# A hybrid decoder layer on one core: operand preparation moved between pairs, and a norm factor computed on GpSimd

## The chip, the cores and the metric

The kernel runs on one core of one Trainium2 chip. The metric is the device time of one execution in microseconds, and the time of a kernel is the median of several runs. A profiled execution is taken beside the timed runs; its trace gives the start and the duration of each instruction on each engine: PE (TensorE matmuls), PEld (TensorE weight loads), DVE (VectorE), ACT (ScalarE), POOL (GpSimd) and SP (SyncE, which only issues transfers here).

## The reference, cut to what matters

One layer over 1024 tokens of width 1024, all in float32. Three root-mean-square norms stand inside it and one behind it; between the first projection and `w_out` lie a pooling mixer and a gated recurrence, which the change doesn't touch:

```
def rms_norm(x, g):
    xf = x.astype(jnp.float32)
    y = xf * lax.rsqrt(jnp.mean(xf * xf, axis=-1, keepdims=True) + RMS_EPS)
    return (y * g.astype(jnp.float32)).astype(x.dtype)

z = rms_norm(h, norm_mix_g[l]);  proj = z @ w_in[l]
...
h = h + jnp.concatenate([y_pool, y_lru], axis=-1) @ w_out[l]
z = rms_norm(h, norm_mlp_g[l])
h = h + jnp.square(jax.nn.relu(z @ w_up[l])) @ w_down[l]
z = rms_norm(h, norm_ple_g[l])
gate = jax.nn.sigmoid(z @ w_ple_gate[l] + b_ple_gate[l])
h = h + gate * (p[l] @ w_ple_proj[l])
return rms_norm(h, norm_final_g)
```

## The kernel before, in words

Activations lie transposed: 128 features on the partitions, 1024 tokens along a row, in eight row blocks `H[0]` to `H[7]`. Each float32 product is made of three matmuls: every operand is split into a high part and a low part (`split`, L189 on ACT for the high part, L190 on DVE for the low part), and high by high, high by low and low by high are accumulated (`mm`, matmuls at L447).

**The up projection** uses a fast matrix multiplication with seven products (named P1 to P7) per pair of output blocks, `m` = 0 to 15 being the pairs. From pair 4 on, two of the seven products are themselves replaced by a second level of the same scheme, over two neighbouring pairs: `up_double(m, k)`, whose small products are issued by `sub_product` (L1020), with names `ps_z_u`, `ps_v_u` and `ps_x_u`. The second level needs sums and differences of quarters of its second operand. They depend on the tokens only, so each is made once: `double_operand(k, n)` builds number `n` for product `k`, with three additions of 128x512 on DVE (L983, L986, inside `total`) and a split. For `k` = "P2" number 2 goes on from the result of number 1, number 4 from that of number 2, and number 3 stands alone; their tiles are `y_wide` (number 4) and `x` (the others). The table `MADE` (L1099) says in which pair each number is made:

```
MADE = {"P4": {1: (3,), 2: (1, 2), 3: (4,)}, "P2": {3: (3, 1), 4: (2, 4)}}
```

`double_operands(m)` is called once in each pair and reads it. The weights of a pair are split one after another ahead of their products: tiles `wu_P` (first level) and `wu_d` and `wu_l` (second level). `wu_sums_raw` holds sums of weights.

**The gate stage** behind the down projection (products `ps_P_d`) works on the first 512 tokens, then on the second 512. Product `o` of the gate is 24 matmuls (`ple_gate`, tile `ps_e`), its projection 6 (`ple_proj`, tile `ps_j`, or a second half of `ps_e`). `ple_out` multiplies the gate product by the norm's factor `R` (tile `rstd`, L1455), applies a sigmoid on ACT (L1456), multiplies by the projection (L1459), and adds to `H[o]` (L1460).

**The norms** (class `Norm`): `add` squares a block on ACT (L491) and adds it up on DVE (L492). `gather` transposes the sums on DVE (L506), reduces them (L507) and splits the result into a high and a low part (L508, L509, tile `sums`). `sums` adds them over the partitions with one small matmul (L519). `rstd` makes the factor from it: a copy and an addition on DVE (L528, L529), a square root on ACT (L533), a reciprocal on DVE (L534) and a transposition that spreads the factor over the tile `rstd` (L535). The norm of the gate has two halves: `first_sums` for the first 512 tokens (matmul result `n_ps`), and the call at L1661 for the second (`n2b_ps`), issued in the round of the gate's product 3. `finish` does the last norm of the first 512 tokens.

**The last norm of the second 512 tokens** is computed by blocks of 128 tokens. There the factor is made by GpSimd's power: `inverse` raises a 128x1 tile to -0.5 (L1590).

The order of the work on each engine is set when the kernel is built: a scheduler lists the instructions by priority, and each engine then runs its own list strictly in that order, waiting on semaphores. `tc.issue_after(ins)` keeps the scheduler from placing an instruction before another one; `pin` and `keep_in_program_order` keep written order.

Of the kernel before, what the change touches and what calls it, by code (L numbers as in the profile page):

```python
# [8 lines left out]
F32 = mybir.dt.float32  # L9
# [3 lines left out]
ALU = mybir.AluOpType  # L13

P = 128
# [49 lines left out]
def block_kernel(  # L65
# [17 lines left out]
    nc = tc.nc  # L83
    pool = ctx.enter_context(tc.tile_pool(name="pool", bufs=1))
# [4 lines left out]
    def fixed(name, dt):  # L89
        return pool.tile([P, S], dt, name=name)  # L90
# [23 lines left out]
    R = fixed("rstd", F32)  # L114
# [17 lines left out]
    spread = edge.tile([P, 72], F32, name="edge")  # L132
# [29 lines left out]
    def turns(z):  # L162
        return z.rearrange("p (a j) -> p j a", a=2)
# [11 lines left out]
    def col(name, i):  # L175
        c = COLS[name] + i
        return vecs[:, c : c + 1]
# [255 lines left out]
    def weights():  # L433
        ask()
        return asked.pop(0)

    def mm(parts, whi, wlo, zhi, zlo, first, last, only=None, more=False, held=False):
        outs = [
            (slice(hs.start + n, hs.start + min(n + HALF, w)), ps[:, n : min(n + HALF, w)])
            for hs, ps in parts  # L440
            for w in (hs.stop - hs.start,)
            for n in range(0, w, HALF)
            if only is None or hs.start + n == only.start
        ]
        for w, z in ((whi, zhi), (whi, zlo), (wlo, zhi)):
            for hs, ps in outs:
                ins = nc.tensor.matmul(  # L447
                    ps, w, turns(z[:, hs]),
                    start=first and z is zhi and w is whi,
                    stop=last and w is wlo,  # L450
                    skip_group_check=more,
                )
                if held:
                    tc.keep_in_program_order(ins)
                    held = False
# [17 lines left out]
    same = pool.tile([P, P], F32R, name="same")  # L473
    eps = pool.tile([P, 1], F32, name="eps")
    nc.scalar.activation(eps, one[:, :1], AF.Copy, scale=EPS)

    class Norm:

# [41 lines left out]
            in_order.clear()  # L520
            return [(hs, o)]

        def rstd(self, out, parts, square=False):


            for hs, o in parts:
                few = self.few(hs)
                nc.vector.tensor_copy(few, o[:, :16])  # L528
                nc.vector.tensor_tensor(few, few, o[:, 16:], ALU.add)  # L529
                if square:  # L530
                    nc.vector.tensor_scalar(few, few, 1.0 / D, EPS, ALU.mult, ALU.add)
                else:
                    nc.scalar.activation(few, few, AF.Sqrt, bias=eps, scale=1.0 / D)  # L533
                nc.vector.reciprocal(few, few)  # L534
                nc.vector.transpose(out[:, hs], few.unsqueeze(2).broadcast_to([P, 16, 32]))  # L535

    def tables():
# [45 lines left out]
    norm = Norm("n0", T[0], T[1:3])  # L583
# [6 lines left out]
    for k in range(NT):  # L590
# [41 lines left out]
        if k < 2:  # L632

            zhi, zlo = A[k]
            for hs in HALVES:
# [4 lines left out]
                for n, o in kinds:  # L640
                    w, z = ((whi, zhi), (whi, zlo), (wlo, zhi))[n]
                    at, ps = next(x for x in places[o] if x[0].start <= hs.start < x[0].stop)
                    ps = ps[:, hs.start - at.start :][:, :HALF]
# [159 lines left out]
    ps = project(3)  # L803
# [4 lines left out]
    ps = project(4)  # L808
# [3 lines left out]
    ps = project(5)  # L812
# [15 lines left out]
    norm = Norm("n1", T[4], T[5:])  # L828
# [10 lines left out]
    for o in range(NT):  # L839
# [15 lines left out]
        ps = out_ps[o]  # L855
# [240 lines left out]
        finish_up(m, cc)  # L1096
        leave_up()

    MADE = {"P4": {1: (3,), 2: (1, 2), 3: (4,)}, "P2": {3: (3, 1), 4: (2, 4)}}  # L1099

    def double_operands(m):

        for k, ns in MADE.items():
            for n in ns.get(m, ()):
# [272 lines left out]
    Z, ple, late, quad = [], [], [], []  # L1377
# [26 lines left out]
    norm2 = Norm("n2", T[0], T[1:2])  # L1404
# [2 lines left out]
    open_proj()  # L1407

    def first_sums(norm=norm2):
        norm.rstd(R, norm.sums(FIRST, pinned=True))  # L1410

    norm2 = Norm("n2b", T[0], T[1:3])


    fin = Norm("n3", T[0], T[1:3])
    rfin = T[5]
    gate_p, held = {}, []
    ms = spread[:, 40 : 40 + 4 * NTOK]
    early_mean, means, inverses = ([ms[:, 4 * x + i : 4 * x + i + 1] for i in range(NTOK)] for x in range(3))
    power = pool.tile([P, 1], F32, name="power")  # L1420
    tc.keep_in_program_order(nc.vector.memset(power, -0.5))

    def ple_psum(g, hs, o, apart):
        turn.append(o)
# [45 lines left out]
    def finish(os):  # L1470

        if 0 in os:
            fin.rstd(rfin, fin.sums(FIRST, fin.tmp[0][:, FIRST]))
        for o in os:
            hv = H[o][:, FIRST]
            nc.vector.scalar_tensor_tensor(hv, hv, col("g_fin", o), rfin[:, FIRST], ALU.mult, ALU.mult)
            if o % 4 == 3:
                store(slice(o - 3, o + 1))

    row = t_all[:, 1:3].rearrange("p a s -> p (a s)")  # L1480
    g_row, b_row, square = row[:, :S], row[:, S : S + NQUAD], row[:, S + NQUAD :]
# [147 lines left out]
    for g, hs in enumerate(GROUPS):  # L1629
        if g == 1:  # L1630
            leave("ple")
            late[:] = space("late", 8, F32)
        for n, o in enumerate(ORDER[g]):
            pg, pj = ple_psum(g, hs, o, False)
            if g == 0 and n < 2:
                ple_gate(g, hs, o, pg, n == 1)
                held.append((o, pg, pj))
                if n == 0:
                    first_sums()
                    continue  # L1640
                for o, pg, pj in held:
                    ple_proj(hs, o, pj)
                for o, pg, pj in held:
                    ple_out(hs, o, pg, pj)
            else:
                ple_proj(hs, o, pj)
                ple_gate(g, hs, o, pg)
            if g == 0 and 1 <= n < 5:
                raw = wp.tile([P, S], F32, tag="raw", name=f"wg0_{n + 3}_raw")
                nc.sync.dma_start(raw, w_gate[n + 3])  # L1650
                x = slice((n - 1) * P, n * P)
                split(raw.rearrange("p (k x) -> p k x", k=NT), *(w[:, :, x] for w in quad))
            if g > 0 or n > 1:
                ple_out(hs, o, pg, pj, g == 0)
            if g == 0 and n > 0:
                for o in range(NT) if n == 1 else ():
                    norm2.add(H[o], SECOND)
                if n == 2:
                    norm2.gather(SECOND, T[2][:, SECOND])
                if n == 3:  # L1660
                    norm2.rstd(R, norm2.sums(SECOND))  # L1661
                for o in LATER[n - 1]:
                    ple_in_normed(o, SECOND)
            if g == 1:
                for j in range(2):
                    turn_block(o, j)
                if n < 2:
                    for x in range(4, NT):
                        turn_block(x, n)
                    turn_out(1, n)  # L1670
                    for i in range(2):
                        turn_in(1, 2 * n + i)
                if n == 3:
                    for j in range(2):
                        turn_out(0, j, (nc.sync, nc.scalar)[j])
                    for i in range(NTOK):
                        turn_in(0, i)
                finish(DONE[n])
                if n == 1:
                    nc.sync.dma_start(row[:, : S + NQUAD], rows.broadcast_to([P, S + NQUAD]))  # L1680
# [127 lines left out]
```

## Time and profile before

| | us |
|---|---|
| median of 3 runs (lowest, highest) | 913.8 (913.64, 914.05) |
| profiled execution | 914.14 |
| its span in the trace | 912.4 |
| PE busy | 903.5 (99%) |
| DVE busy | 742.0 (81%) |
| ACT busy | 517.3 (57%) |
| POOL busy | 51.8 (6%) |

The span is the time from the first to the last instruction of the trace; the profiled execution is 1.74 us longer than its span. A row of the timeline gives start, duration, engine, line, operation, output<-input, the shape, a count where neighbouring instructions are merged, and in brackets the idle time of the engine ahead of the instruction with what ended it. Instructions of one engine overlap a little: a duration includes the run-out of the pipeline, so the pace of an engine is read from the starts. Starts show 0.60 us per 128x512 addition on DVE where the row says 0.68 or 0.69.

### The profile page before, as it was taken

What the parts mean: (1) busy time and instruction counts of PE and PEld (TensorE: products, weight loads), DVE (VectorE), ACT (ScalarE), POOL (GpSimd) and SP (SyncE); (2) the same over time, 40 slices, a digit from 0 to 9 for tenths busy, and PEclk for the clock granted to TensorE, in tenths of its full rate; (3) what the DMA queues carried; (4) which work ended last, traced back from release to release, by engine and by line L of the source; (5) the groups of instructions that cost most, each with busy time, mean ns of one, the idle gap of its engine ahead of it and who ended that gap; (6) DMA issues with size and microseconds to landing.
All of it is one profiled execution on the core that took longest, in us unless ns stands there. A gap on an engine that the chain in (4) does not pass through costs nothing.

```text
span 912.4 us, 11874 instructions
## 1 busy us (share of the span) xinstructions
PE 903.5 (99%) x4419; PEld 792.5 (87%) x4419; DVE 742.0 (81%) x1015; ACT 517.3 (57%) x688; POOL 51.8 (6%) x76
## 2 busy tenths in 40 slices
PE   9999999999999999999999999999999999999996
PEld 7888888888888899999998888888888888888886
DVE  7999974668977987887887978699787679899876
ACT  6569892447565666766767554463443436475323
POOL 4300001000000000000000000000001001100001
PEclk9999999999999999999999999999999999999999
DMA  7311145435477488687684988456635355332353
GB/s 274 103 47 34 59 153 148 151 92 173 117 217 225 125 246 203 194 242 198 190 243 170 352 322 285 146 193 207 199 111 145 116 173 117 57 115 70 99 170 136
DMA packets 60330, 150.90 MB, mean 165 GB/s; under 512 B 5360, under 2 KB 10352, under 8 KB 60272
## 3 DMA queue, kind: packets, MB, share of 16 engines
q1 hardware_dynamic: 54288, 136.77, 45.6%
q0 software_dynamic: 4752, 12.59, 8.3%
q10 hardware_dynamic: 1232, 0.79, 0.4%
q8 instruction: 35, 0.57, 0.2%
q14 instruction: 23, 0.19, 0.1%
HBM read 110.27 MB, written 39.85 MB: 165 GB/s over the span
## 4 chain that ended last, share of the span: by engine, by line
PE 92%; DVE 4%; issue 2%; DMA 1%; ACT 0%; POOLq 0%; POOL 0%; ACTq 0%; DVEq 0%
PE ps_P_d L447 31%; PE ps_i L447 9%; PE ps_o L447 9%; PE ps_d_u L447 8%; PE ps_b_u L447 8%; PE ps_a_u L447 5%; PE ps_e L447 5%; PE ps_z_u L1020 3%; PE ps_l L447 3%; PE ps_P_u L447 3%; PE ps_e L1541 2%; PE ps_v_u L1020 2%; PE ps_l L644 1%; PE ps_x_u L1020 1%; PE ps_g L713 1%
## 5 line engine op out<-in xcount | busy, mean ns | idle before, releaser
L447 PE MATMUL ps_P_d<-a,wd_P_hi 128*128 128x512 f32 x880 | 261.7, 379 | 0.0
L447 PEld LDWEIGHTS ps_P_d<-a,wd_P_hi 128*128 128x128 f32 x880 | 166.3, 189 | 23.6
L447 PE MATMUL ps_P_d<-a,wd_P_lo 128*128 128x512 f32 x440 | 166.8, 379 | 0.0
L447 PEld LDWEIGHTS ps_P_d<-a,wd_P_lo 128*128 128x128 f32 x440 | 83.2, 189 | 11.8
L447 PE MATMUL ps_b_u<-a,wu_P 128*128 128x512 f32 x360 | 82.6, 379 | 0.0
L222 DVE TENSOR_TENSOR t_h<-t_h 128x512 f32<-128x512 f32 (+2 forms) x104 | 72.6, 708 | 11.6 <-ACT t_h L925 10.4
L190 DVE TENSOR_TENSOR wu_P<-t_h,wu_P 128x512 fp32r<-128x512 f32 x84 | 57.4, 686 | 27.8 <-ACT wu_P L189 27.6
L447 PEld LDWEIGHTS ps_b_u<-a,wu_P 128*128 128x128 f32 x360 | 66.4, 189 | 8.4
L190 DVE TENSOR_TENSOR a<-wd,a 128x1024 fp32r<-128x1024 f32 x56 | 67.3, 1220 | 2.6 <-ACT a L189 2.3
L447 PE MATMUL ps_i<-a,wi_hi 128*128 128x512 f32 x256 | 66.1, 381 | 0.0
L189 ACT ACTIVATE wu_P<-t_h 128x512 fp32r<-128x512 f32 x84 | 52.2, 624 | 22.3 <-DVE t_h L222 11.9
L189 ACT ACTIVATE a<-wd 128x1024 fp32r<-128x1024 f32 x56 | 58.6, 1052 | 10.0 <-PE ps_P_d L447 6.5
L899 DVE TENSOR_TENSOR t_h<-t_h,ps_P_d 128x512 f32<-128x512 f32 (+1 forms) x48 | 37.1, 773 | 30.5 <-PE ps_P_d L447 30.5
L447 PE MATMUL ps_a_u<-y_wide,wu_P 128*128 128x512 f32 x240 | 55.1, 379 | 0.0
L447 PEld LDWEIGHTS ps_i<-a,wi_hi 128*128 128x128 f32 x256 | 48.1, 189 | 8.0 <-PE ps_g L713 0.3
L189 ACT ACTIVATE wd_P_hi<-wd 128x1024 fp32r<-128x1024 f32 x24 | 25.3, 1055 | 50.2 <-PE ps_P_d L447 47.7
L447 PEld LDWEIGHTS ps_a_u<-y_wide,wu_P 128*128 128x128 f32 x240 | 45.3, 189 | 6.4
L447 PE MATMUL ps_d_u<-a,wu_P 128*128 128x512 f32 x180 | 41.6, 380 | 0.1
L447 PE MATMUL ps_d_u<-y,wu_P 128*128 128x512 f32 x180 | 41.3, 379 | 0.0
L447 PE MATMUL ps_i<-a,wi_lo 128*128 128x512 f32 x128 | 38.1, 379 | 0.0
L190 DVE TENSOR_TENSOR wd_P_lo<-wd,wd_P_hi 128x1024 fp32r<-128x1024 f32 x24 | 29.3, 1221 | 10.1 <-ACT wd_P_hi L189 10.1
L447 PEld LDWEIGHTS ps_d_u<-a,wu_P 128*128 128x128 f32 x180 | 33.1, 189 | 4.7 <-DVE wu_P L190 0.5
(307 smaller groups left out, 1749.8 us busy)
## 6 DMA issues: line engine op xcount, KB each, us to landing
wd<-act SPq DMA_DIRECT2D x56, 512.0 KB, 5.5
act<-t_h SPq DMA_DIRECT2D x48, 512.0 KB, 4.9
t_h<-in_w_up SPq DMA_DIRECT2D x30, 512.0 KB, 5.0
wd<-in_w_down SPq DMA_DIRECT2D x16, 512.0 KB, 5.8
t_h<-in_w_up POOLq DMA_DIRECT2D x15, 512.0 KB, 7.8
t_h<-in_xT SPq DMA_DIRECT2D x14, 512.0 KB, 4.6
wg_raw<-in_w_gate SPq DMA_DIRECT2D x10, 512.0 KB, 3.3
wi_raw<-in_w_in SPq DMA_DIRECT2D x9, 512.0 KB, 3.3
```

Source lines behind the costliest of these rows:

```text
L189: first = pin(nc.scalar.activation(hi, src, AF.Copy))
L190: lowest[:] = [pin((eng or nc.vector).tensor_tensor(lo, src, f32(hi), ALU.subtract)).ins]
L222: return nc.vector.tensor_tensor(to, x, y, op).ins
L447: ins = nc.tensor.matmul(ps, w, turns(z[:, hs]), start=first and z is zhi and w is whi, stop=last and w is wlo, skip_group_check=more,)
L644: nc.tensor.matmul(ps, kblk(w, o), turns(z[:, hs]), start=k == n == 0, stop=False)
L713: nc.tensor.matmul(x, w[r, o * P : (o + 1) * P], turns(z[r, at : at + HALF]), start=n == 0, stop=n == 2)
L899: (eng or nc.vector).tensor_tensor(to, to if y is None else y, x, ALU.add)
L1020: nc.tensor.matmul(ps, kblk(w, t), turns(z[:, t]), start=t == x == 0 and not more, stop=t == 1 and x == 2, skip_group_check=more,)
L1541: nc.tensor.matmul(pg, z, turns(quad[x == 1][:, k]), start=n == 0, stop=n == 3 * NT - 1, skip_group_check=True)
```

## The change

Three edits.

1. In `MADE`, the operands for "P2" are made in pairs 2, 3 and 4 (number 3; then 1 and 2; then 4), where they were made in pairs 3 and 4 (3 and 1; then 2 and 4). P4's are unchanged.
2. `rstd` gets a switch `late`, used for both halves of the gate's norm and for the last norm's first half. With it the factor is not made by ACT's square root and DVE's reciprocal but by one DVE instruction (multiply and add, 128x16) and GpSimd's power with exponent -0.5 (128x16). The exponents stand in sixteen columns that GpSimd fills at the start; the single column that DVE filled at L1421 is gone.
3. The matmul of the second half's sums is held behind the last matmul that had been written so far, the last one of the gate's product 3 (the fourth gate product).

```diff
+    latest = []
@@ mm
                     skip_group_check=more,
                 )
+                latest[:] = [ins.ins]
                 if held:
@@ setup
+    powers = spread[:, 53:69]
+    nc.gpsimd.memset(powers, -0.5)
@@ Norm
-        def rstd(self, out, parts, square=False):
+        def rstd(self, out, parts, square=False, late=False):
             for hs, o in parts:
                 few = self.few(hs)
                 nc.vector.tensor_copy(few, o[:, :16])
                 nc.vector.tensor_tensor(few, few, o[:, 16:], ALU.add)
-                if square:
+                if square or late:
                     nc.vector.tensor_scalar(few, few, 1.0 / D, EPS, ALU.mult, ALU.add)
                 else:
                     nc.scalar.activation(few, few, AF.Sqrt, bias=eps, scale=1.0 / D)
-                nc.vector.reciprocal(few, few)
+                if late:
+                    nc.gpsimd.tensor_tensor(few, few, powers, ALU.pow)
+                else:
+                    nc.vector.reciprocal(few, few)
                 nc.vector.transpose(out[:, hs], few.unsqueeze(2).broadcast_to([P, 16, 32]))
@@
-    MADE = {"P4": {1: (3,), 2: (1, 2), 3: (4,)}, "P2": {3: (3, 1), 4: (2, 4)}}
+    MADE = {"P4": {1: (3,), 2: (1, 2), 3: (4,)}, "P2": {2: (3,), 3: (1, 2), 4: (4,)}}
@@ gate stage
-        norm.rstd(R, norm.sums(FIRST, pinned=True))
+        norm.rstd(R, norm.sums(FIRST, pinned=True), late=True)
-    power = pool.tile([P, 1], F32, name="power")
-    tc.keep_in_program_order(nc.vector.memset(power, -0.5))
+    power = powers[:, :1]
@@ finish
-            fin.rstd(rfin, fin.sums(FIRST, fin.tmp[0][:, FIRST]))
+            fin.rstd(rfin, fin.sums(FIRST, fin.tmp[0][:, FIRST]), late=True)
@@ round of product 3
-                    norm2.rstd(R, norm2.sums(SECOND))
+                    with tc.issue_after(latest[0]):
+                        ps = norm2.sums(SECOND)
+                    norm2.rstd(R, ps, late=True)
```

The edits move instructions in three places. In the changed kernel the lines up to L434 keep their numbers and the later ones are a few higher (L986 is L994, L492 is L497, L509 is L514, L535 is L543).

**Place 1: DVE in pair 4**, from the low part of P5's weight (`wu_P_2373`, in the changed kernel `wu_P_2378`) to the sums of weights. L986 and L994 are operand additions, L222 additions on weights, `x` the low part of an operand, `wu_d` the low part of a second-level weight. Before:

```order
L190 TENSOR_TENSOR wu_P_2373<-t_h,wu_P_2373 128x512
L986 TENSOR_TENSOR t_h<-t_h,y_wide 128x512
L222 TENSOR_TENSOR t_h<-t_h 128x512
L986 TENSOR_TENSOR t_h<-t_h,y_wide 128x512
L222 TENSOR_TENSOR t_h<-t_h 128x256
L190 TENSOR_TENSOR wu_P_2409<-t_h,wu_P_2409 128x512
L190 TENSOR_TENSOR x_1776<-t_h,x_1776 128x512
L190 TENSOR_TENSOR wu_d_2392<-t_h,wu_d_2392 128x512
```

With the change:

```order
L190 TENSOR_TENSOR wu_P_2378<-t_h,wu_P_2378 128x512
L994 TENSOR_TENSOR t_h<-t_h,y_wide 128x512
L222 TENSOR_TENSOR t_h<-t_h 128x512
L222 TENSOR_TENSOR t_h<-t_h 128x256
L190 TENSOR_TENSOR x_1778<-t_h,x_1778 128x512
L222 TENSOR_TENSOR t_h<-t_h 128x256
L190 TENSOR_TENSOR wu_P_2414<-t_h,wu_P_2414 128x512
L190 TENSOR_TENSOR wu_d_2397<-t_h,wu_d_2397 128x512
```

One operand addition is gone from between the two weights, and an addition of 128x256 that stood behind `wu_d` has come ahead of it.

**Place 2: DVE at the first half's factor.** `edge` holds the 16 sums, `wg_2_lo` and `a` are low parts of gate weights. Before:

```order
L528 COPY edge<-n_ps_6529 128x16
L190 TENSOR_TENSOR wg_2_lo<-wg_2_raw,wg_2_hi 128x1024
L529 TENSOR_TENSOR edge<-edge,n_ps_6529 128x16
L190 TENSOR_TENSOR a<-wg_4_raw,a 128x8x128
L492 TENSOR_TENSOR t_h<-t_h 128x512
L534 RECIPROCAL edge<-edge 128x16
L492 TENSOR_TENSOR t_h<-t_h 128x512
L535 STREAM_TRANSPOSE rstd<-edge 128x512
L492 TENSOR_TENSOR t_h<-t_h 128x512
L1455 TENSOR_TENSOR t_h<-ps_e_0_6497,rstd 128x512
```

With the change:

```order
L533 COPY edge<-n_ps_6528 128x16
L190 TENSOR_TENSOR wg_2_lo<-wg_2_raw,wg_2_hi 128x1024
L534 TENSOR_TENSOR edge<-edge,n_ps_6528 128x16
L190 TENSOR_TENSOR a<-wg_4_raw,a 128x8x128
L536 TENSOR_SCALAR edge<-edge 128x16
L497 TENSOR_TENSOR t_h<-t_h 128x512
L543 STREAM_TRANSPOSE rstd<-edge 128x512
L497 TENSOR_TENSOR t_h<-t_h 128x512
L1462 TENSOR_TENSOR t_h<-ps_e_0_6496,rstd 128x512
```

One addition of squares stands between the new instruction and the transposition, which waits for GpSimd's power; the addition that stood in the old gap comes later.

**Place 3: DVE and PE at the second half's sums.** On DVE, before:

```order
L1455 TENSOR_TENSOR t_h<-ps_e_2_6609,rstd 128x512
L506 STREAM_TRANSPOSE t_h<-t_h 128x512
L507 TENSOR_REDUCE edge<-t_h 128x16
L1459 TENSOR_TENSOR t_h<-t_h,ps_j_2_6610 128x512
L508 CAST sums_6229<-edge 128x16
L1460 TENSOR_TENSOR t_h<-t_h 128x512
L509 TENSOR_TENSOR sums_6229<-edge,sums_6229 128x16
L190 TENSOR_TENSOR a<-wg_6_raw,a 128x8x128
L492 TENSOR_TENSOR t_h<-t_h 128x512
```

With the change:

```order
L1462 TENSOR_TENSOR t_h<-ps_e_2_6608,rstd 128x512
L497 TENSOR_TENSOR t_h<-t_h 128x512
L511 STREAM_TRANSPOSE t_h<-t_h 128x512
L1466 TENSOR_TENSOR t_h<-t_h,ps_j_2_6609 128x512
L512 TENSOR_REDUCE edge<-t_h 128x16
L1467 TENSOR_TENSOR t_h<-t_h 128x512
L513 CAST sums_6230<-edge 128x16
L190 TENSOR_TENSOR a<-wg_6_raw,a 128x8x128
L497 TENSOR_TENSOR t_h<-t_h 128x512
L514 TENSOR_TENSOR sums_6230<-edge,sums_6230 128x16
```

The low part of the sums, which the small matmul reads, now stands behind a split of a gate weight and one more addition of squares. On PE, before (the last matmul of gate product 3, the small matmul, the first of projection 4):

```order
L447 MATMUL ps_e0_3_6661<-ple6_6239,wg0_3_lo_6619 128x512
L447 MATMUL ps_e0_3_6661<-ple6_6239,wg0_3_hi_6618 128x512
L447 MATMUL ps_e0_3_6661<-ple7_6240,wg0_3_hi_6618 128x512
L447 MATMUL ps_e0_3_6661<-ple6_6239,wg0_3_lo_6619 128x512
L519 MATMUL n2b_ps512_6708<-sums1_6229,same_162 128x32
L447 MATMUL ps_j0_4_6722<-proj0_6475,proj4_6479 128x512
```

With the change:

```order
L449 MATMUL ps_e0_3_6660<-ple6_6240,wg0_3_lo_6618 128x512
L449 MATMUL ps_e0_5_6768<-proj0_6476,proj4_6480 128x512
L449 MATMUL ps_e0_5_6768<-proj1_6477,proj4_6480 128x512
L449 MATMUL ps_e0_5_6768<-proj0_6476,proj5_6481 128x512
L449 MATMUL ps_e0_5_6768<-proj2_6478,proj6_6482 128x512
L449 MATMUL ps_e0_5_6768<-proj3_6479,proj6_6482 128x512
L524 MATMUL n2b_ps512_6707<-sums1_6230,same_162 128x32
L449 MATMUL ps_j0_4_6721<-proj0_6476,proj4_6480 128x512
```

Five of the six matmuls of projection 5 now stand between the last matmul of gate product 3 and the small matmul.

## The prediction

> **What bounds the kernel now.** I read the head of the page, then the waits of TensorE, then the timeline around each wait, then the chain of waits.
>
> ```profile
> span 912.4 us, 11874 instructions
> PE 903.5 (99%) x4419; PEld 792.5 (87%) x4419; DVE 742.0 (81%) x1015; ACT 517.3 (57%) x688; POOL 51.8 (6%) x76
> ...
> PE ps_l L589 <- PEq L1794: 0.8, 1, 0.8
> PE n2b_ps L519 <- DVE sums L509: 0.6, 1, 0.6
> PE ps_z_u L1020 <- DVE wu_d L190: 0.2, 1, 0.2
> ```
>
> TensorE sets the end. Its whole waiting is three waits: the start, which the change leaves alone, and one at each place that the change touches. The matmul count stays, so only these two waits and the hidden losses beside them can move the time. Pair 4 loses more than its row of 0.2 says:
>
> ```profile
> 294.34 2.75 PE L447 MATMUL ps_a_u<-y_wide,wu_P 128*128 128x512 f32 x12
> ...
> 297.60 3.13 PE L447 MATMUL ps_d_u<-a,wu_P 128*128 128x512 f32 x12
> ...
> 301.29 0.49 PE L1020 MATMUL ps_z_u<-x,wu_d 128*128 128x256 f32 x2
> ...
> 302.25 0.71 PE L1020 MATMUL ps_z_u<-x,wu_d 128*128 128x256 f32 x4 [0.25 <-DVE wu_d L190]
> ...
> 305.17 0.83 PE L1020 MATMUL ps_x_u<-a,wu_d 128*128 128x256 f32 x6
> ...
> 313.03 2.75 PE L447 MATMUL ps_a_u<-y_wide,wu_P 128*128 128x512 f32 x12
> ```
>
> and in the chain of waits the same product of the next two pairs (start, length):
>
> ```profile
> 313.19 2.59 PE ps_a_u L447 x12
> ...
> 330.83 2.59 PE ps_a_u L447 x12
> ```
>
> From one `ps_a_u` to the next, pair 4 takes 313.03 - 294.34 = 18.69 us, the next pair 330.83 - 313.19 = 17.64 us. So pair 4 loses 1.05: 0.38 in `ps_d_u` (3.13 against 2.75), 0.62 from 301.29 to 305.17 (3.88 us for six small matmuls at 0.112 and twelve at 0.216, 3.26), the rest beside them.
>
> The gate stage, around the second half's sums:
>
> ```profile
> 821.06 0.59 PE L447 MATMUL ps_e<-ple,wg_hi 128*128 128x512 f32 x2
> ...
> 826.99 0.28 PE L519 MATMUL n2b_ps<-sums,same 128*128 128x32 f32 x1 [0.58 <-DVE sums L509]
> 827.12 1.54 PE L447 MATMUL ps_j<-proj,proj 128*128 128x512 f32 x6
> 828.50 0.81 PE L447 MATMUL ps_e<-ple,a 128*128 128x512 f32 x3
> ```
>
> Gate product 3 is 24 matmuls at 0.216, so it is through at 821.06 + 5.18 = 826.24. The small matmul starts at 826.99: TensorE loses 0.75 there, and with the small matmul itself 0.97 (828.50 - 826.24, less 1.29 for projection 4). What it waits for is VectorE, which works through its list here without a gap:
>
> ```profile
> 805.08 4.63 DVE L190 TENSOR_TENSOR proj<-t_h,proj 128x1024 fp32r<-128x1024 f32 x4 [1.12 <-ACT proj L189]
> ...
> 809.66 0.06 DVE L1421 MEMSET power<- 128x1 f32 x1
> ...
> 810.86 0.17 DVE L529 TENSOR_TENSOR edge<-edge,n_ps 128x16 f32<-128x16 f32 x1
> 810.94 1.22 DVE L190 TENSOR_TENSOR a<-wg_raw,a 128x1024 fp32r<-128x1024 f32 x1
> 812.07 0.68 DVE L492 TENSOR_TENSOR t_h<-t_h 128x512 f32<-128x512 f32 x1
> 812.67 0.25 DVE L534 RECIPROCAL edge<-edge 128x16 f32<-128x16 f32 x1
> 812.84 0.65 DVE L492 TENSOR_TENSOR t_h<-t_h 128x512 f32<-128x512 f32 x1
> ...
> 826.77 0.17 DVE L509 TENSOR_TENSOR sums<-edge,sums 128x16 fp32r<-128x16 f32 x1
> 826.85 1.23 DVE L190 TENSOR_TENSOR a<-wg_raw,a 128x1024 fp32r<-128x1024 f32 x1
> 827.99 0.68 DVE L492 TENSOR_TENSOR t_h<-t_h 128x512 f32<-128x512 f32 x1
> ```
>
> The reader is to see that no row after 805.08 carries an idle time: from there to the sums at 826.94 VectorE is the chain, and anything put ahead of the sums makes TensorE's wait longer by its whole length.
>
> **Edit 1, the operands: -0.14.** Place 1 in the order shows what counts. The loss in `ps_d_u` hangs on P5's weight:
>
> ```profile
> 288.74 1.42 DVE L222 TENSOR_TENSOR t_h<-t_h 128x512 f32<-128x512 f32 x2 [1.39 <-ACT t_h L925]
> ...
> 297.56 0.69 DVE L190 TENSOR_TENSOR wu_P<-t_h,wu_P 128x512 fp32r<-128x512 f32 x1
> ...
> 301.51 0.68 DVE L190 TENSOR_TENSOR wu_d<-t_h,wu_d 128x512 fp32r<-128x512 f32 x1
> ```
>
> VectorE last stands idle ahead of 288.74 (for ScalarE's squares, which the edit doesn't touch). From there to P5's weight its list has the same fourteen instructions before and with the change, another operand's addition taking the place of the one moved forward. The weight comes at 297.56 again, and the 0.38 stays. Between it and `wu_d` an operand addition (0.60) leaves and a 128x256 addition (0.34) enters: `wu_d` comes 0.26 sooner. The matmuls that wait for it start at 301.99; four small ones (0.45) and now twelve of `ps_b_u` (2.59; one of them used to fill the gap) end at 305.03, against 305.17: 0.14 gained. The work moved forward, three additions and a split, lands in pair 2's end and pair 3's start, where VectorE is busy 13.07 of 18.10 us:
>
> ```profile
> 276.20:294.30 18.10, 18.10 (x85) 15.86 (x84) 13.07 (x21) 10.56 (x17) 0.88 (x1) 1.00 0.71 204
> ```
>
> The third busy number is VectorE's: 5 us are free, so the move costs nothing there. Bounds: 0, and the whole loss of 1.05.
>
> **Edits 2 and 3, the second sums: +0.51 and a wait for the power.** Place 3: five matmuls of projection 5 stand ahead of the small matmul, so TensorE reaches it at 826.24 + 1.08 = 827.32. On VectorE the split of a gate weight (826.85 to 827.99, 1.14) and one more addition of squares (0.60) now stand ahead of the sums; the reciprocal (0.17) and the memset (0.06) are gone, the multiply-and-add (0.08, as L529's start to the next) is new. Net 1.59, so the sums end at 826.94 + 1.59 = 828.53, and TensorE, 0.05 later (826.94 to 826.99 now), has waited 1.26 instead of 0.75: +0.51. That is without any wait in place 2.
>
> In place 2 VectorE has only one addition (0.60) to do between the multiply-and-add and the transposition that needs the power. The multiply-and-add starts at 812.05 (812.07 less the memset's 0.02), ends at 812.22 like other 128x16 instructions, and VectorE is free for the transposition at 812.05 + 0.08 + 0.60 = 812.73. No row shows a power of 16 columns. Those of one column are:
>
> ```profile
> 892.38 0.69 DVE L1527 TENSOR_TENSOR late<-late,t_h 128x512 f32<-128x512 f32 x1
> ...
> 892.54 0.95 POOL L1590 TENSOR_TENSOR edge<-edge,power 128x1 f32<-128x1 f32 x1 [99.84 <-DVE edge L1517]
> ...
> 901.94 0.55 POOL L1590 TENSOR_TENSOR edge<-edge,power 128x1 f32<-128x1 f32 x1 [4.45 <-DVE edge L1517]
> ```
>
> and a plain two-input instruction of four columns:
>
> ```profile
> 14.40 0.20 POOL L564 TENSOR_TENSOR sp<-sp 128x4 f32<-128x4 f32 x1
> ```
>
> A power takes 0.55, and 0.95 with a VectorE addition beside it, as there will be here. With 0.08 to reach POOL and 0.04 back, 812.22 + 0.08 + 0.95 + 0.04 = 813.29: VectorE stands for 0.56 even if fifteen more columns are free. At the other end every column costs what one costs beyond a plain instruction, 0.55 - 0.20 = 0.35, and the wait is 0.56 + 15 x 0.35 = 5.8. Part of the 0.35 is surely paid once per instruction; I take a sixth of it, 0.06 per column, nearer to the low end because four plain columns together take 0.20: a wait of 0.56 + 0.90 = 1.46. All of it delays the sums.
>
> [...]
>
> **What costs nothing, and its cover.** ScalarE loses three square roots and five of six table loads:
>
> ```profile
> 810.33 1.28 ACT L533 ACT_TABLE_LOAD   x1
> 811.63 0.31 ACT L533 ACTIVATE edge<-edge,eps 128x16 f32<-128x16 f32 x1
> ```
>
> But the root was ready at 811.94 and the reciprocal came at 812.67: VectorE's list was the limit, and nothing is gained. The second half's power leaves VectorE standing some 2 us. What hides it is the distance to the second half's operands: the last split of them, and the first product that reads them, and further down the user of two late loads:
>
> ```profile
> 850.78 0.69 DVE L190 TENSOR_TENSOR a<-t_h,a 128x512 fp32r<-128x512 f32 x1
> ```
> ```profile
> 854.56 11.65 PE ps_e L447 x54
> ```
> ```profile
> 900.31 0.69 DVE L1587 TENSOR_TENSOR late<-late,t_h 128x512 f32<-128x512 f32 x1
> ```
>
> That is 3.8 us, and more for the last of the operands, which the product reads last. Without that cover it would cost the 2 us. At the last norm a weight split and a product (1.8 us) stand between the multiply-and-add and the transposition, and TensorE doesn't wait for it. There the output's first store gets ahead of two loads on SP's queue, which then wait for four scalings; their user is the row at 900.31, so some 20 us remain. The memset on POOL at the start is 0.1 to 0.2 us on an engine that then waits for others.
>
> **The sum**: -0.14 + 0.51 + 1.46 = +1.83. The profiled execution would be 914.14 + 1.83 = 916.0; the median shown is 0.34 below the profiled execution, so I state the median: 913.8 + 1.8 = **915.6**.
>
> **The rivals.**
>
> *The power is light*: fifteen columns cost nearly nothing. For it: four columns of a product take 0.20. Against it: a single column of power takes 0.35 more than that. Time: +0.51 + 0.56 - 0.14 = +0.9, 914.7; decided by a power of 128x16 under 1.25 us.
>
> *The power is heavy*, slower: GpSimd works column by column at more than 0.10. For it, the 0.35 of one column. Place: the transposition in place 2 and through it the small matmul. From 0.10 on the wait is over 2.06 and the time over 913.8 + 2.4 = 916.2; at 0.25 it is 918.5.
>
> *The sums are in time*: VectorE reaches them before TensorE reaches 827.32, because ScalarE, free of table loads, lets VectorE run faster, and pair 4's loss vanishes whole. Time: -1.05 - 0.75 = -1.8, 912.0; with only the second part 913.0. Against it: VectorE's rows have no gap that ScalarE could close, and its list is longer by 1.59.
>
> **Chances.** Forecast (0.02 to 0.10 per column, +1.2 to +2.4) 0.45; light 0.22; heavy 0.22; in time 0.11. A measurement of this kernel can tell about 0.2%, 1.83 us, from no change, and the forecast sits on that line: half of it counts as slower. Slower 0.22 + 0.22 = 0.44; within 0.22 + 0.22 + 0.06 = 0.50; faster 0.06, half of the last rival. The range: 914.0 below (the light power with part of pair 4's loss regained), 918.5 above (0.25 per column).
>
> **What would show it.** Right: the wait of `n2b_ps` for VectorE grows from 0.6 to about 2.7; an idle time of VectorE of about 1.5 ahead of the first `rstd` transposition, released by POOL; a power of 128x16 of 1.5 to 2 us; `ps_d_u` of pair 4 still at 3.1. Wrong: no wait at `n2b_ps`, or a pair 4 of 17.64.

## The result and the profile after

The change made the kernel slower, by far more than predicted.

| | before | changed |
|---|---|---|
| median of the runs (lowest to highest, number) | 913.72 us (913.57 to 914.05, 4) | 920.63 us (919.76 to 921.10, 4) |
| ratio, 95% interval | | 1.0074 (1.0057 to 1.0092) |
| profiled execution, its span | 914.14, 912.4 | 920.78, 918.8 |

Predicted were 915.6 and a range of 914.0 to 918.5; 44% stood on slower by over 0.2%.

The waits of TensorE in the changed kernel (total, how often, the longest):

```profile
PE n2b_ps L524 <- DVE sums L514: 4.3, 1, 4.3
...
PE ps_z_u L1028 <- DVE wu_d L190: 0.4, 1, 0.4
```

The wait at the second half's sums went from 0.6 to 4.3. The timeline of TensorE shows it, and a second loss behind it:

```profile
826.21 1.24 PE L449 MATMUL ps_e<-proj,proj 128*128 128x512 f32 x5
831.71 0.39 PE L524 MATMUL n2b_ps<-sums,same 128*128 128x32 f32 x1 [4.26 <-DVE sums L514]
831.94 2.91 PE L449 MATMUL ps_j<-proj,proj 128*128 128x512 f32 x6
834.64 6.94 PE L449 MATMUL ps_e<-ple,a 128*128 128x512 f32 x24
841.42 0.38 PE L449 MATMUL ps_e<-proj,proj 128*128 128x512 f32 x1
841.63 5.34 PE L449 MATMUL ps_e<-ple,a 128*128 128x512 f32 x24
```

Six matmuls of a projection take 2.70 (834.64 - 831.94) where they took 1.38 before, and the next gate product 6.78 (841.42 - 834.64) where the one after it takes 5.18. The windows of the same trace say why; the last but two number of a row is TensorE's granted clock, the share of its full clock that it was given:

```profile
830.00:831.00 1.00, 0.00 (x0) 0.00 (x0) 1.00 (x2) 0.41 (x1) 0.00 (x0) 1.00 0.00 0
831.00:832.00 1.00, 0.29 (x2) 0.29 (x2) 1.00 (x3) 0.00 (x0) 0.00 (x0) 0.52 0.18 20
832.00:833.00 1.00, 1.00 (x4) 0.82 (x4) 0.68 (x4) 0.71 (x1) 0.17 (x1) 0.50 0.84 229
...
837.00:838.00 1.00, 1.00 (x4) 0.80 (x4) 1.00 (x3) 0.25 (x1) 0.00 (x0) 0.57 0.00 0
838.00:839.00 1.00, 1.00 (x6) 0.89 (x5) 1.00 (x3) 0.97 (x2) 0.00 (x0) 1.00 0.00 0
```

The clock fell to one half shortly after 831.0, while TensorE stood still, and came back before 838.0. In windows of 0.1 us the mean is 0.68 from 831.00 to 831.10 and 0.69 from 837.80 to 837.90, so the edges lie at 831.04 and 837.86: 6.83 us, and TensorE worked in 6.15 of them (from 831.71) at half speed.

The sum of the loss: the small matmul starts 831.71 - 826.99 = 4.72 later, of which five projection matmuls (1.08) are work done early: 3.64. From 831.71 to the 24 matmuls at 841.63 lie the small matmul (0.13 at full clock, as from 826.99 to 827.12 before) and 31 others (6.70), which would have ended at 838.54: 3.09 lost to the clock, and half of the 6.15 is 3.08. Pair 4 gives 0.03 back. Together 6.70, against 920.78 - 914.14 = 6.64.

What made the sums late is in VectorE's timeline:

```profile
812.03 0.17 DVE L536 TENSOR_SCALAR edge<-edge 128x16 f32<-128x16 f32 x1
812.11 0.69 DVE L497 TENSOR_TENSOR t_h<-t_h 128x512 f32<-128x512 f32 x1
815.63 0.71 DVE L543 STREAM_TRANSPOSE rstd<-edge 128x512 f32<-128x512 f32 x1 [2.84 <-POOL edge L540]
...
819.77 0.69 DVE L497 TENSOR_TENSOR t_h<-t_h 128x512 f32<-128x512 f32 x1
820.60 0.69 DVE L1466 TENSOR_TENSOR t_h<-t_h,ps_j 128x512 f32<-128x512 f32 x1
...
831.48 0.17 DVE L514 TENSOR_TENSOR sums<-edge,sums 128x16 fp32r<-128x16 f32 x1
```

and GpSimd's:

```profile
812.28 3.31 POOL L540 TENSOR_TENSOR edge<-edge 128x16 f32<-128x16 f32 x1 [19.62 <-DVE edge L536]
832.83 2.91 POOL L540 TENSOR_TENSOR edge<-edge 128x16 f32<-128x16 f32 x1 [17.23 <-DVE edge L536]
873.62 2.89 POOL L540 TENSOR_TENSOR edge<-edge 128x16 f32<-128x16 f32 x1 [37.88 <-DVE edge L536]
```

The power of 16 columns takes 2.9 to 3.3 us, and VectorE stands 2.84 ahead of the transposition. The sums start 831.48 - 826.77 = 4.71 later: 1.59 from the longer list, as predicted; 2.92 from this stall, taken from the starts (815.63 - 812.11 less the addition's 0.60; the row's 2.84 leaves out the run-out of the addition); some 0.23 ahead of 820.60, where VectorE's addition of 0.6 is through at 820.37 and the next instruction needs a sigmoid that ScalarE, itself fed late, gives only then; less the 0.03 from pair 4.

### The profile page after: what moved, and what is told of

Its sections match the earlier page's. It is cut to its first block, busy times and chain, and to the rows that moved or that the text cites. A ratio compares the mean times of both kernels' runs of the same rounds, so it can differ in the third digit from the quotient of the medians.

```text
span 918.8 us, 11862 instructions
## 1 busy us (share of the span) xinstructions
PE 906.3 (99%) x4419; PEld 794.7 (86%) x4419; DVE 741.7 (81%) x1014; ACT 510.3 (56%) x680; POOL 61.0 (7%) x80
## 4 chain that ended last, share of the span: by engine, by line
PE 92%; DVE 4%; issue 2%; ACT 1%; POOL 0%; DMA 0%; POOLq 0%; ACTq 0%; DVEq 0%
PE ps_P_d L449 30%; PE ps_i L449 9%; PE ps_o L449 9%; PE ps_b_u L449 8%; PE ps_d_u L449 8%; PE ps_e L449 5%; PE ps_a_u L449 5%; PE ps_z_u L1028 3%; PE ps_l L449 3%; PE ps_P_u L449 3%; PE ps_e L1548 2%; PE ps_v_u L1028 2%; PE ps_l L652 1%; PE ps_x_u L1028 1%; PE ps_j L449 1%
## 5 line engine op out<-in xcount | busy, mean ns | idle before, releaser
L222 DVE TENSOR_TENSOR t_h<-t_h 128x512 f32<-128x512 f32 (+2 forms) x104 | 72.6, 708 | 11.6 <-ACT t_h L933 10.4
L496 ACT ACTIVATE t_h<-t_h 128x512 f32<-128x512 f32 (+1 forms) x35 | 27.5, 795 | 22.2 <-DVE t_h L497 11.9
```

Of the source, the lines that this page charges most:

```text
L222: return nc.vector.tensor_tensor(to, x, y, op).ins
L496: pin(nc.scalar.activation(sq, t[:, hs], AF.Square))
```

## The experiments

The theory after the traces: the first half's power alone delays the sums; TensorE stands still long enough for its clock to fall; edit 1, the hold and the two other powers change nothing that can be told. The rivals: the hold or another power shares the loss; the slow matmuls behind the wait have another cause than the standing still.

The kernel before was timed again beside each experiment and took 914.49 to 914.64 there instead of 913.72. So each run is compared with before beside it, while the expectations in us rest on 913.7 and 920.6.

**Edit 1 alone.**

```diff
--- before
-    MADE = {"P4": {1: (3,), 2: (1, 2), 3: (4,)}, "P2": {3: (3, 1), 4: (2, 4)}}
+    MADE = {"P4": {1: (3,), 2: (1, 2), 3: (4,)}, "P2": {2: (3,), 3: (1, 2), 4: (4,)}}
```

> The kernel before with edit 1 alone (the operands in pairs 2 to 4). Theory (the sum's first term, with the 0.03 that pair 4 gained in the changed kernel, 18.66 against 18.69): no difference that can be told, 913.7, P5's weight late as before (ps_d_u 3.1 in pair 4). Rival (edit 1 costs by itself, by VectorE's fuller pairs 2 and 3): over 915.

Measured: 914.57 (before, on the same chip, 914.64), ratio 1.000 (0.999 to 1.001). Pair 4, from one `ps_a_u` at 294.75 to the next at 313.39, takes 18.64. On TensorE's timeline:

```profile
298.00 3.13 PE L447 MATMUL ps_d_u<-a,wu_P 128*128 128x512 f32 x12
...
302.39 0.71 PE L1020 MATMUL ps_z_u<-x,wu_d 128*128 128x256 f32 x4 [0.36 <-DVE wu_d L190]
```

P5's weight is as late as before. Edit 1 is worth some 0.05 us, which no timing here can tell.

**The changed kernel without the first half's power.**

```diff
--- changed
-        norm.rstd(R, norm.sums(FIRST, pinned=True), late=True)
+        norm.rstd(R, norm.sums(FIRST, pinned=True))
```

> The changed kernel with the square root and the reciprocal again in the first half's factor; edit 1, the hold and the two other powers stay. Theory (the first power alone delays the sums): the wait of n2b_ps is back at 0.6 or less, the granted clock stays 1.00 there, 913.7 to 914.0. Rival (the second half's power, during which VectorE stands 3.0, is on the path too): 916 or more.

Measured: 914.16, ratio 0.9993 (0.9983 to 1.0002), and the clock is 1.00 throughout. TensorE, GpSimd and VectorE around the second half's sums, a timeline each:

```profile
827.19 0.28 PE L524 MATMUL n2b_ps<-sums,same 128*128 128x32 f32 x1 [0.53 <-DVE sums L514]
```
```profile
830.05 2.94 POOL L540 TENSOR_TENSOR edge<-edge 128x16 f32<-128x16 f32 x1 [37.10 <-DVE edge L536]
```
```profile
833.03 0.72 DVE L543 STREAM_TRANSPOSE rstd<-edge 128x512 f32<-128x512 f32 x1 [3.06 <-POOL edge L540]
```

Without the first power the loss is gone whole. The second power makes VectorE stand just as long (3.06), and it costs nothing: the cover that the prediction named is there.

**The first half's power alone.**

```diff
--- before
+    powers = spread[:, 53:69]
+    nc.gpsimd.memset(powers, -0.5)
...
-        norm.rstd(R, norm.sums(FIRST, pinned=True))
+        norm.rstd(R, norm.sums(FIRST, pinned=True), late=True)
```

(with `late` in `rstd` as in the change).

> The kernel before with the first half's power alone: no edit 1, no hold, square roots elsewhere. Theory: the whole loss of the changed kernel, 920.6, with a wait of 4.3 at n2b_ps, five projection matmuls ahead of it, and a granted clock near 0.5 for some 6 us after it. Rival (the hold places the small matmul behind, and the other powers share the loss): under 918.5, no five matmuls ahead.

Measured: 920.22 (before 914.64), ratio 1.0059 (1.0044 to 1.0074). TensorE's timeline and two windows:

```profile
825.88 1.24 PE L447 MATMUL ps_e<-proj,proj 128*128 128x512 f32 x5
831.36 0.39 PE L522 MATMUL n2b_ps<-sums,same 128*128 128x32 f32 x1 [4.23 <-DVE sums L512]
```
```profile
828.00:830.00 2.00, 0.00 (x0) 0.00 (x0) 2.00 (x5) 1.52 (x2) 0.00 (x0) 0.86 0.00 0
...
836.00:837.00 1.00, 1.00 (x6) 0.89 (x4) 1.00 (x2) 0.41 (x1) 0.00 (x0) 0.87 0.00 0
```

The wait is there whole, with the five matmuls ahead of the small one though nothing holds it. In finer windows the clock falls at 829.44 and rises at 836.26: 6.83 us again, but only 4.90 of them fall on work (from 831.36), 2.45 lost instead of 3.08.

**The changed kernel without the hold.**

```diff
--- changed
-                    with tc.issue_after(latest[0]):
-                        ps = norm2.sums(SECOND)
-                    norm2.rstd(R, ps, late=True)
+                    norm2.rstd(R, norm2.sums(SECOND), late=True)
```

> The changed kernel without the hold: the second half's small matmul is asked for as in the kernel before. Theory (the order in which the instructions are issued comes from the first power; the hold changes nothing, as the listing of every engine's instructions is the same with and without it): 920.6, five projection matmuls ahead of the small one, a wait of 4.3. Rival (the hold puts the small matmul behind): no five matmuls ahead, and a wait of 5.3.

Measured: 919.93 (919.70 to 920.50), ratio to before 1.0062 (1.0049 to 1.0076). TensorE's timeline:

```profile
826.65 1.24 PE L449 MATMUL ps_e<-proj,proj 128*128 128x512 f32 x5
832.19 0.40 PE L524 MATMUL n2b_ps<-sums,same 128*128 128x32 f32 x1 [4.30 <-DVE sums L514]
...
840.47 0.38 PE L449 MATMUL ps_e<-proj,proj 128*128 128x512 f32 x1
```

The hold moves nothing: the instructions of each engine stand in the same order in the trace with it and in the trace without it, and with the hold but without the first power (above) no projection matmul stands ahead of the small one. What moved the five matmuls is the first power. From 832.19 to 840.47 lie the small matmul and 30 others, 6.61 at full clock, so the clock costs 1.67 in this execution. The edges of the low clock, in windows of 0.1 us:

```profile
832.00:832.10 0.10, 0.00 (x0) 0.00 (x0) 0.10 (x3) 0.00 (x0) 0.00 (x0) 0.64 0.00 0
...
835.40:835.50 0.10, 0.10 (x1) 0.06 (x1) 0.00 (x0) 0.10 (x1) 0.10 (x1) 0.80 0.00 0
```

It fell at 832.03, only 0.16 before TensorE went back to work, and rose at 835.44: 3.41 us, half of the 6.83 of the other two. With nearly the same wait the clock's price is 1.67, 2.45 and 3.08 in the three traces, by when in the wait it falls and how long it stays low. Against before beside it this kernel is 5.44 slower, the changed kernel 6.91, with the same instructions in the same order; so the 1.5 between them, and the 1.3 by which the first power alone (5.58) stays under the changed kernel, say nothing about the edits.

**Work in the wait (e4_filled).**

```diff
--- changed
                     with tc.issue_after(latest[0]):
-                        ps = norm2.sums(SECOND)
+                        both = bank("n2b_ps512")
+                        for x in range(20):
+                            hi, lo, wh, wl = ple[0]
+                            tc.keep_in_program_order(
+                                nc.tensor.matmul(both[:, 32:], kblk(wh, 0), hi[:, :480], start=True, stop=True)
+                            )
+                        ps = norm2.sums(SECOND, into=both, pinned=True)
```

> The changed kernel with 20 matmuls of 128x480 (work whose result nothing reads) between the third gate product and the small matmul, so that TensorE stands still some 1.5 instead of 4.3 while the sums come at the same time, 831.65. Projection 5's five matmuls go behind it, which costs 5 x 0.216 = 1.1. Theory (the clock falls because TensorE stood still): granted clock 1.00, the 3.0 of the slow matmuls saved, 920.6 + 1.1 - 3.0 = 918.7. Rival (the matmuls behind it are slow for another reason, GpSimd's second power or their operands): 920.6 + 1.1 = 921.7 and a granted clock near 0.5 as before.

Measured: 919.52 (919.29 to 919.81). That is 4.88 above before beside it (914.64); the theory's 918.7 was 5.0 above 913.7, the rival's 921.7 8.0 above. TensorE's timeline and a window:

```profile
825.88 4.50 PE L1673 MATMUL n2b_ps<-proj,proj 128*128 128x480 f32 x20
831.43 0.28 PE L524 MATMUL n2b_ps<-sums,same 128*128 128x32 f32 x1 [1.04 <-DVE sums L514]
831.56 1.54 PE L449 MATMUL ps_j<-proj,proj 128*128 128x512 f32 x6
```
```profile
832.00:833.00 1.00, 1.00 (x7) 0.86 (x6) 0.24 (x1) 0.72 (x1) 0.00 (x0) 1.00 0.84 287
```

The sums come no sooner, the clock stays at 1.00, and the projection takes 1.38 again. The fall of the clock is caused by the standing still. GpSimd's second power is no rival either: the run with the first power alone has no second one, and its matmuls were slow. What is left is the lateness of the sums: the small matmul stands 831.43 - 825.88 = 5.55 behind the gate product instead of 0.75, 4.8 more, and the profiled executions differ by 919.29 - 914.14 = 5.15; the rest was not traced.

**Less work in the wait.** The same with `range(14)`.

> As e4_filled with 14 matmuls in the wait instead of 20, so that TensorE stands still 2.3 us. In the traces the clock stayed low for 6.83 us, twice 3.41, and fell 3.60 us after the last matmul in the changed kernel, but 2.3 after it with the first power alone. [...]

Measured: the profiled execution took 1611.62 us at a mean clock of 0.557, so nothing of this wait can be read from its trace. The three others took 918.99, 919.06 and 920.60 with mean clocks of 0.998, 0.998 and 0.997; kernels without a long wait have 0.997 to 0.999 too. So whether a wait of 2.3 us in all can be enough stays open.

**Half of the power (e8).**

```diff
--- changed
-                    nc.gpsimd.tensor_tensor(few, few, powers, ALU.pow)
+                    nc.gpsimd.tensor_tensor(few[:, :8], few[:, :8], powers[:, :8], ALU.pow)
```

> The changed kernel with GpSimd's power on 8 of the 16 columns only, in all three norms; the other 8 keep the mean square in place of the factor, so half of the tokens' output is not the reference's. Theory (the clock falls only when TensorE stands still long enough, and 4.26 is beyond that point): the power takes 1.25 less, the wait at n2b_ps is 3.0, the granted clock stays at 1.00, and the time is 920.6 - 1.25 - 3.0 = 916.4. Rival (the loss of the clock goes with the length of the wait): 920.6 - 1.25 - 0.9 = 918.5, and a granted clock under 1 behind the wait.

Measured: 917.29, 917.90, 919.22 and 919.80, median 918.56, ratio 1.0044 (1.0031 to 1.0058). The profiled execution is the first, 917.29. GpSimd and TensorE in it:

```profile
831.94 1.65 POOL L540 TENSOR_TENSOR edge<-edge 128x8 f32<-128x8 f32 x1 [17.23 <-DVE edge L536]
```
```profile
830.82 0.28 PE L524 MATMUL n2b_ps<-sums,same 128*128 128x32 f32 x1 [3.00 <-DVE sums L514]
830.95 1.54 PE L449 MATMUL ps_j<-proj,proj 128*128 128x512 f32 x6
```

The wait is the 3.00 expected, and in this execution the clock does not fall. In the four executions the mean clock is 0.998, 0.996, 0.997 and 0.995, in the order of the times; the twelve executions with a wait of 4.2 to 4.3 (the changed kernel, the first power alone, no hold) have 0.995 or 0.996 each. So neither expectation holds as written: at 3.0 us the fall seems to come in some executions and not in others. That is read from mean clocks, since only the execution without a fall left a trace. The median meets the rival's 918.5 by chance: the four times spread over 2.5 us, and 918.5 rests on a before that is 0.8 faster.

**The price of a power.**

```diff
--- before
                     first_sums()
+                    expo, data = spread[:, 53:69], spread[:, :16]
+                    nc.gpsimd.memset(expo, -0.5)
+                    for op in (ALU.pow, ALU.mult):
+                        for x in (1, 2, 4, 8, 16):
+                            nc.gpsimd.tensor_tensor(data[:, :x], data[:, :x], expo[:, :x], op)
```

> The kernel before with ten instructions more on GpSimd, behind the first half's transposition, whose result nothing reads: powers of 1, 2, 4, 8 and 16 columns, then products of the same widths. Theory (every column costs the same, (2.9 - 0.55) / 15 = 0.16): powers of 0.55, 0.71, 1.02, 1.65 and 2.9 us, more where VectorE's additions run beside, and products of 0.2 or less. Rival (a fixed dear start, then cheap columns): all powers from 2 columns on near 2.5.

Measured, GpSimd's timeline in windows of one instruction each:

```profile
814.95 0.93 POOL L1644 TENSOR_TENSOR edge<-edge 128x1 f32<-128x1 f32 x1 [21.54 <-DVE rstd L535]
815.96 0.70 POOL L1644 TENSOR_TENSOR edge<-edge 128x2 f32<-128x2 f32 x1
816.74 1.37 POOL L1644 TENSOR_TENSOR edge<-edge 128x4 f32<-128x4 f32 x1
818.19 1.67 POOL L1644 TENSOR_TENSOR edge<-edge 128x8 f32<-128x8 f32 x1
819.94 2.90 POOL L1644 TENSOR_TENSOR edge<-edge 128x16 f32<-128x16 f32 x1
```

A power of n columns takes 0.39 + 0.157 n: that gives 0.55, 0.70, 1.02, 1.65 and 2.90. Two rows, those of 1 and 4 columns, took 0.38 and 0.35 more. In VectorE's timeline each of them begins inside an addition of two SBUF tiles (tiles with `ps` in their names lie in PSUM, where TensorE leaves its results, the others in SBUF):

```profile
814.79 0.65 DVE L492 TENSOR_TENSOR t_h<-t_h 128x512 f32<-128x512 f32 x1
...
816.56 0.67 DVE L492 TENSOR_TENSOR t_h<-t_h 128x512 f32<-128x512 f32 x1
```

The additions end, by the starts of the next rows, at 815.36 and 817.15, some 0.4 after the power's start: what the power takes longer is about what was left of them. The other three began beside a product that reads PSUM (2 and 16 columns) or 0.1 before the end of a split (8 columns). The same holds for the first half's power, 3.31 instead of 2.9, which began at 812.28 inside the addition of 812.11. That GpSimd waits for that rest was not tested apart.

Products cost next to nothing per column: one of 16 columns took 0.2 (the two 128x16 instructions together 3.1). Those of 2 and 4 columns took 0.53 each, more than expected; each began inside such an addition. The time, 914.95 in one execution, lies within before's (913.59 to 916.29). The theory's line holds, the rival's flat price does not.

**The small matmul moved behind projection 5.** The wait before the change is itself worth 0.75, and the runs had shown that neither the hold nor the power moves the small matmul to where it waits for nothing. So it was asked for there:

```diff
--- before
-                if n == 3:
-                    norm2.rstd(R, norm2.sums(SECOND))
-                for o in LATER[n - 1]:
-                    ple_in_normed(o, SECOND)
+                for x in LATER[n - 1] if n != 3 else ():
+                    ple_in_normed(x, SECOND)
...
                 ple_proj(hs, o, pj)
+                if g == 0 and n == 4:
+                    with tc.issue_after(latest[0]):
+                        ps = norm2.sums(SECOND)
+                    norm2.rstd(R, ps)
+                    for x in LATER[2]:
+                        ple_in_normed(x, SECOND)
                 ple_gate(g, hs, o, pg)
```

First with edit 1 (c1_sums_later):

> The kernel before with edit 1, square roots and reciprocals throughout, and the second half's small matmul moved behind projection 5's six matmuls (the hold set on the last of them, and the factor and the first two operands asked for there). Theory (before, TensorE loses 0.75 because the sums come at 826.94 and gate product 3 is through at 826.24; six matmuls fill 1.3): no wait at n2b_ps, 0.75 gained and 0.04 in pair 4, ratio 0.9991. Rival (the factor comes 0.5 later and the second half's operands with it, so the wait shows up at the second half's first product): ratio 1.000 or more.

Measured: 913.35 (before 914.49), ratio 0.9990 (0.9982 to 0.9999). TensorE's timeline:

```profile
825.96 1.46 PE L449 MATMUL ps_j<-proj,proj 128*128 128x512 f32 x6
827.25 0.18 PE L522 MATMUL n2b_ps<-sums,same 128*128 128x32 f32 x1
827.28 5.43 PE L449 MATMUL ps_e<-ple,a 128*128 128x512 f32 x24
```

No wait, and even the small matmul's own 0.13 (826.99 to 827.12) shrinks to 0.03. Then without edit 1:

> The kernel before with the second half's small matmul behind projection 5's six matmuls and nothing else changed (c1_sums_later without edit 1). Theory (that place alone brings c1's gain, edit 1 none): ratio 0.9990 to 0.9994, no wait at n2b_ps, pair 4 as before at 18.69. Rival (c1's gain came from both edits together, or from none): ratio 0.9995 or more.

Measured: 913.33 (before 914.49), ratio 0.9991 (0.9982 to 1.0000). The waits of TensorE have no row for `n2b_ps` any more. The two runs agree: moving the small matmul brings about 0.1%, edit 1 nothing. It is the fastest version of this study, by less than the 0.2% that the prediction called measurable, and only by many repeats.

**The operands earlier still.** As the first of these two, with

```diff
-    MADE = {"P4": {1: (3,), 2: (1, 2), 3: (4,)}, "P2": {2: (3,), 3: (1, 2), 4: (4,)}}
+    MADE = {"P4": {1: (3,), 2: (1, 2), 3: (4,)}, "P2": {2: (3, 1), 3: (2, 4)}}
```

> As c1_sums_later, with all four of the second operand's parts in pairs 2 and 3 (parts 3 and 1 in pair 2, 2 and 4 in pair 3), none in pair 4. Theory (pair 4 loses 1.05 because VectorE is busy all through it): P5's weight comes sooner, ps_d_u takes 2.75, and up to 1.0 more is gained, ratio 0.9980 to 0.9991. Rival (the work that moves delays weights in pairs 2 and 3, or is queued ahead of P5's weight again): ratio 0.9991 or more.

Measured: 914.47, ratio 0.9999 (0.9990 to 1.0008): it gives away what the small matmul had gained. TensorE's timeline in pair 4:

```profile
298.70 0.60 PE L449 MATMUL ps_d_u<-a,wu_P 128*128 128x512 f32 x2
300.31 2.43 PE L449 MATMUL ps_d_u<-a,wu_P 128*128 128x512 f32 x10 [1.01 <-DVE wu_P L190]
```

P5's weight comes later than before, not sooner, as the rival had it. VectorE's timeline has the operands' instructions ahead of pair 4's weights now, from 283 to 294; that they are the cause was not tested apart.

## Why the prediction was wrong

**Right.** What bounds the kernel; that VectorE is the chain from 805 to the sums, so that whatever stands ahead of them is paid in full; the 1.59 of the longer list and the five matmuls worth 1.08; that the transposition would stand for GpSimd and for nothing else; that the second power (VectorE stands 3.06 without the first), the last norm, ScalarE's lost table loads and the queues would cost and bring nothing, as far as the run without the first power shows (0.9993, at most 1.0002).

**The price of the power, the first step that failed.** The term was 0.56 + 15 columns x 0.06 = 1.46, nearer to the low end of the bounds "because four plain columns together take 0.20". A plain product is no measure for a power: its 16 columns take 0.2 in all, while every column of a power costs 0.157. With that the stall is 0.56 + 15 x 0.157 = 2.92, as measured from the starts. It was inside the bounds (0 to 0.35); the rival of the heavy power, with a chance of 0.22, is the one that came. Both rows of the power of one column, 0.55 and 0.95, had been quoted; the error was to let an instruction of another operation choose the place between the ends.

**The clock, the step that was missing.** With the right price the sum would have been -0.14 + 0.51 + 2.92 = 3.3, that is 917.1, still 3.5 short, and the range's upper end rested on the same sum. The prediction treated a wait of TensorE as costing its own length. Here a wait of 4.26 costs 3.08 more in slow matmuls, and the run with the wait filled (1.04 of standing still, granted clock 1.00) shows that the standing still is the cause. In the traces the low clock is half of the full one (0.50), for 6.83 us in the changed kernel, 6.83 with the first power alone and 3.41 without the hold: two of the stretches are twice the third. In the changed kernel 78.51, about 23 times 3.41, lie between the rise at 837.86 and the fall at the kernel's end (916.37, from a mean of 0.84 in the window from 916.30 to 916.40). What sets these lengths no run tested.

Nor does the length of the wait alone say whether the clock falls. With the first power alone it fell at 829.44, 2.3 us after TensorE had stopped at 827.1. With half of the power TensorE stood still longer than that, 3.00 from 827.82 to 830.82, and in the one trace the clock stayed at 1.00; the mean clocks of the other executions (0.996, 0.997 and 0.995) suggest that the same wait brought a fall in some of them. That it matters at which moment the wait begins is the author's estimate from this; what decides the fall and the rise, no run shows.

The rival of the heavy power should have carried this: somewhere between a wait of 1.04 us, which cost no clock, and one of 4.2, its price was not a slope but a step.

**A smaller miss on the path:** 0.23 where VectorE waits for a sigmoid at 820.60. The prediction let VectorE's list move as a block; ScalarE, fed late by the stalled VectorE, comes back with its own split (1.04 from 817.49) and table load (1.28 from 818.55) in the way.

**Edit 1.** Predicted was a gain of 0.14; the changed kernel's pair 4 gained 0.03 (18.66 against 18.69):

```profile
297.60 3.14 PE L449 MATMUL ps_d_u<-a,wu_P 128*128 128x512 f32 x12
...
302.00 0.71 PE L1028 MATMUL ps_z_u<-x,wu_d 128*128 128x256 f32 x4 [0.36 <-DVE wu_d L190]
302.54 2.76 PE L449 MATMUL ps_b_u<-a,wu_P 128*128 128x512 f32 x12
305.13 0.83 PE L1028 MATMUL ps_x_u<-a,wu_d 128*128 128x256 f32 x6
```

`wu_d` lets its matmuls start at 302.00 (predicted 301.99), and P5's weight keeps its 0.38, both as worked out. The four small matmuls then take 0.54 to the next product, not 0.45 (before the change they took 0.55, from 302.25 to 302.80), so what comes behind them ends 0.1 later than summed: the term was mis-sized by that 0.1, and it is too small to be told in a time.

**The hold.** The prediction charged the move of the small matmul to edits 2 and 3 together. It belongs to edit 2 alone; edit 3 does nothing. That changed no number.

## What to carry to other kernels

A wait on the engine that sets the end has two prices, its length and, on TensorE, the clock that falls when it gets long: here 1 us cost 1 us and 4.3 us cost 6.0 to 7.3; of 3 us the one trace shows no fall, while the mean clocks of other executions suggest one. A root moved to GpSimd's power saved ScalarE table loads (five of the gate stage's six, 1.28 us each) but took 0.39 us and 0.157 more per column with nothing else to hide it, so the question is who waits for the result, not which engine is free. To remove a short wait of a small matmul, put work that is ready ahead of it (0.1% here); a hold that the order already satisfied moved nothing (the same order and a wait of 4.3 with and without it).

## What the runs showed of the hardware

- GpSimd's power costs 0.157 us per column beyond 0.39, while a product of 16 columns takes 0.2. A power that began inside a VectorE addition of two SBUF tiles took about 0.4 longer (0.93 against 0.55, 3.31 against 2.91), about as long as was left of that addition; that the one causes the other was not tested.
- TensorE's granted clock fell to 0.50 in the wait of 4.2 to 4.3 us in all three traces, 2.3, 3.6 and 4.1 us after TensorE stopped, and stayed there for 6.83, 6.83 and 3.41, though TensorE was back at work for 4.90, 6.15 and 3.25 of them. With 1.04 us of standing still it did not fall, and in the one trace with 3.00 it did not either.
